# A hybrid decoder block on one core: the first weights' low part in two halves, the fourth early column tile whole

## The chip, the cores and the metric

The kernel runs on one core of a Trainium2 chip. A core has engines that run side by side, each with its own queue of instructions: PE (TensorE) multiplies matrices, DVE (VectorE), ACT (ScalarE) and POOL (GpSimd) work element by element, and SP (SyncE) issues transfers. They wait for each other by semaphores. PE loads 128x128 weights (shown as PEld) and streams the other operand past them; its results go to PSUM, which has banks of 128x512 floats.

The metric is the device time of one execution in microseconds (us); the median of several runs counts.

## The reference

One decoder block with 512 tokens, width 1024, in float32. What is computed, cut to what matters:

```
h = rmsnorm(x, norm1_g)
z = h @ w_in + b_in                                # 1024 x 6656
z_glu, z_rx, z_rg, z_ga, z_gb = split(z)           # 2048, 1280, 1280, 1024, 1024
u = z_glu[:, :1024] * sigmoid(z_glu[:, 1024:])
u = silu(layernorm(causal_depthwise_conv(u, 31 taps)))
y_a = u @ conv_w_out + conv_b_out
xb = causal_depthwise_conv(z_rx, 4 taps)
hb = rg_lru(xb, lru_wa, lru_ba, lru_wx, lru_bx, lru_lambda)   # linear recurrence over the tokens
y_b = (hb * gelu(z_rg)) @ lru_w_out
x = x + (sigmoid(z_ga) * y_a + sigmoid(z_gb) * y_b) @ w_mix_out
h = rmsnorm(x, norm2_g)
x = x + (silu(h @ ffn_w1) * (h @ ffn_w3)) @ ffn_w2             # inner width 2816
out = rmsnorm(x, norm_f_g)
```

The change touches only the first two lines: the normed rows, and the first four column tiles of `z`.

## The kernel before

**Products in three parts.** A float32 operand is split into a high part, rounded to the type that PE multiplies fast (float32r), and a low part, the rest (`split_to`, L131: a copy, then a subtraction at L129). A product is the sum of three matmuls: high weights by high tokens, high weights by low tokens, low weights by high tokens (`mm3`, L530). With `lo_last` all matmuls of the third kind come last.

**Weights.** A column tile of `w_in` is 128 columns wide and 1024 deep, so it has eight pieces of 128x128, numbered c = 0 to 7, side by side in one 128x1024 tile. `wchunk` lists such chunks in the order of use. `load_chunk` issues the transfer into one of four raw buffers (L158); `emit_chunk` (L161) makes the high part and the low part in one of five `hl` buffers, both of them in one tile `hl[P, 2, 1024]`. The high part is made by ACT, for the first chunk by DVE (L172, shown as L133). The low part is made by POOL (L129), for the second chunk by DVE.

**The early stage** (L638 to L669) is under `manual_schedule`: the instructions of PE, ACT, DVE and SP stay in the order in which they are written. POOL's order there, and everything after L669, comes from a planner that goes by its own estimates of when an instruction is ready. The four row tiles of `x` (128 tokens each) are normed (`norm1_rows`, L606), turned by PE (`turn_rows`, L586) and split into high and low parts h1c with norm1_g applied (`turned_parts`, L592: ACT makes the high, DVE the low part of tile c, for 256 tokens at once). While the second half of the tokens is still being prepared, PE already multiplies the first half with four column tiles, those numbered 0, 8, 1 and 9 (`EARLY_IN`; here called in0, in8, in1, in9; they make the first two glu channels). `early_mm(i, hf)` is the product of the i-th of these tiles with half `hf` of the tokens, 24 matmuls of 256 columns, into half of the PSUM bank `z{m}`. The first of them, `early_mm(0, 0)`, has its 24 matmuls in an order written out by hand (L626 and L627, matmuls at L632), because its operands are being made while it runs; the others go through `mm3`. After the four first halves, `rows_turned` (L519) turns the rows of the small parameters, and the four second halves follow.

**After it.** A string of small DVE operations works out the softplus of `lru_lambda` and scaled biases from those parameter rows (L677 to L699, with one Exp on ACT at L680). Then `ORDER` (L226) sets the sequence of the input products, whole column tiles with 24 matmuls of 512 columns, and DVE runs the long convolution beside them (`run_beside`, L789). `glu` takes its early results from `ready`. There are six PSUM banks for products and two for other things.

Of the kernel before, what the change touches and what calls it, by code (L numbers as in the profile page):

```python
# [8 lines left out]
F32 = mybir.dt.float32  # L9
# [17 lines left out]
ND = D // P  # L27
# [69 lines left out]
def tile_block(ctx, tc, a, out):  # L97
# [15 lines left out]
    def pairt(name, dtype=F32R):  # L113

        return longt(f"{name}h", dtype), longt(f"{name}l", dtype)

    def bank(name):
        return psum.tile([P, T], F32, tag="mm", name=name)
# [4 lines left out]
    vec, act, pe, pool_e = nc.vector, nc.scalar, nc.tensor, nc.gpsimd  # L123


    newest = {}

    def sub(eng, o, x, y):
        return eng.tensor_tensor(out=o, in0=x, in1=y, op=ALU.subtract)  # L129

    def split_to(h, l, full, eng, copy=act.copy):  # L131

        copy(h, full)  # L133
        last = sub(eng, l, full, h.bitcast(F32))
        if eng is pool_e:
            newest["sub"] = last.ins
        return h, l
# [8 lines left out]
    emitted = [0]  # L146
# [5 lines left out]
    def load_chunk(i):  # L152
        key, src, kt, cols = chunks[i][:4]
        raw = raws.tile([P, 1024], F32, tag="raw", name=f"raw_{key}")
        if callable(src):
            src(raw)
        else:
            newest["load"] = newest["any"] = nc.sync.dma_start(raw[:, : kt * cols].rearrange("p (k n) -> p k n", k=kt), src).ins  # L158
        loaded_raw[i] = raw

    def emit_chunk():  # L161
        key, src, kt, cols, where, lo, after = chunks[emitted[0]]
        if emitted[0] not in loaded_raw:
            load_chunk(emitted[0])
        raw = loaded_raw.pop(emitted[0])
        emitted[0] += 1
        n = kt * cols
        rv = raw[:, :n]
        if where == "hl":
            hl = hls.tile([P, 2, 1024], F32R, tag="hl", name=f"hl_{key}")  # L170

            h, l = split_to(hl[:, 0, :n], hl[:, 1, :n], rv, lo, act.copy if emitted[0] > 1 else vec.tensor_copy)  # L172
            if after:
                after(rv, h)
            held[key] = (h.rearrange("p (k n) -> p k n", k=kt), l.rearrange("p (k n) -> p k n", k=kt))
        else:
            held[key] = [
                split_to(longt(f"{key}h{i}", F32R), longt(f"{key}l{i}", F32R), rv[:, i * T : (i + 1) * T], lo)
                for i in range(2)
            ]  # L180

    def emit_to(n):
        while emitted[0] < min(len(chunks), n):
            emit_chunk()

    def weights(key, ahead=AHEAD):
        i = next(i for i, c in enumerate(chunks) if c[0] == key)
        emit_to(i + 1 + ahead)
        return held.pop(key)
# [283 lines left out]
    for name, n in ROWS:  # L473
# [4 lines left out]
        while done < n:  # L478
            m = min(n - done, P - row_at(at + done)[1])
# [5 lines left out]
    def load_rows(i):  # L485
        lo, m, src = parts[i]
        b, r = row_at(lo)
        nc.sync.dma_start(rowt[b][r : r + m, :P], src)
# [4 lines left out]
    def load_x(t):  # L493
        for h in range(2):
            nc.sync.dma_start(xt[t][h], x_nat[:, t, h * T : (h + 1) * T])
# [23 lines left out]
    def rows_turned(c0, c1):  # L519
        pt = bank2(f"par_ps{c0}")  # L520
        for c in range(c0, c1, P):
            m = min(P, c1 - c)
            pe.transpose(pt[:, c - c0 : c - c0 + m], rowt[row_at(c)[0]][:m, :P], ident[:m, :m])
        vec.tensor_copy(par[:, c0:c1], pt[:, : c1 - c0])
# [5 lines left out]
    def mm3(ps, ws, xs, lo_last=False):  # L530


        n = 3 * len(ws)
        i = 0
        three = [((wh, xh), (wh, xl), (wl, xh)) for (wh, wl), (xh, xl) in zip(ws, xs)]
        if lo_last:
            three = [q[:2] for q in three] + [q[2:] for q in three]
        for l, r in (q for qs in three for q in qs):
            pe.matmul(ps, l, r, start=i == 0, stop=i == n - 1)  # L539
            i += 1  # L540

    def w_tiles(key, kt, ahead=AHEAD):
        h, l = weights(key, ahead)
        return [(h[:, k, :], l[:, k, :]) for k in range(kt)]
# [41 lines left out]
    def turn_rows(t, ps):  # L586

        for c in range(ND):
            at = 256 * (c // 4) + P * (t % 2)
            pe.transpose(ps[c % 4][:, at : at + P], xt[t][c // 4][:, (c % 4) * P : (c % 4 + 1) * P], ident)  # L590

    def turned_parts(hf, ps):  # L592
        cs = slice(hf * 256, hf * 256 + 256)
        for c in range(ND):
            g, at = pc("norm1_g", c), 256 * (c // 4)
            p_ = ps[c % 4][:, at : at + 256]
            h, l = (v[:, cs] for v in h1p[c])
            act.activation(h, p_, AF.Copy, scale=g)
            vec.scalar_tensor_tensor(out=l, in0=p_, scalar=g, in1=h.bitcast(F32), op0=ALU.mult, op1=ALU.subtract)

    def parts_of(pair_tiles, cs=slice(0, T)):
        return [(h[:, cs], l[:, cs]) for h, l in pair_tiles]

    h1p = [pairt(f"h1{c}") for c in range(ND)]

    def norm1_rows(t, between=lambda: None):  # L606
        junk = [shortt(f"n1j{t}{h}") for h in range(2)]
        r = rstd_of(xt[t], junk)
        for h in range(2):
            vec.tensor_scalar(out=xt[t][h], in0=xt[t][h], scalar1=r, scalar2=None, op0=ALU.mult)  # L610
            if h == 0:
                between()
# [3 lines left out]
    EARLY_IN = [(GLU + j + 8 * o) for j in range(EARLY) for o in range(2)]  # L616
    early = []

    def early_mm(i, hf):
        m = EARLY_IN[i]  # L620
        if hf == 0:
            early.append((m, w_tiles(f"in{m}", ND, 0), bank(f"z{m}")))
        _, ws, ps = early[i]
        if (i, hf) == (0, 0):

            order = [(m, c) for c in range(5) for m in (0, 1)]  # L626
            order += [(2, 0), (2, 1), (0, 5), (1, 5), (2, 2), (2, 3), (0, 6), (1, 6), (2, 4), (2, 5), (0, 7), (2, 6), (2, 7), (1, 7)]  # L627
            xs = parts_of(h1p, HALVES[0])
            for n, (m, c) in enumerate(order):
                (wh, wl), (xh, xl) = ws[c], xs[c]  # L630
                l, r = ((wh, xh), (wh, xl), (wl, xh))[m]
                pe.matmul(ps[:, HALVES[0]], l, r, start=n == 0, stop=n == len(order) - 1)  # L632
            return
        mm3(ps[:, HALVES[hf]], ws, parts_of(h1p, HALVES[hf]), lo_last=hf == 0)


    ET = mybir.EngineType
    with tc.manual_schedule(engines={ET.PE, ET.Activation, ET.DVE, ET.SP}):  # L638

        turned = [bank(f"tx0{q}") for q in range(4)]  # L640
        norm1_rows(0)
        turn_rows(0, turned)
        norm1_rows(1, lambda: rows_turned(0, n_first))
        emit_to(1)
        turn_rows(1, turned)
        turned_parts(0, turned)
        emit_to(2)
        load_x(2)
        load_x(3)
        load_chunk(2)  # L650
        load_chunk(3)
        norm1_rows(2)
        early_mm(0, 0)
        early_mm(1, 0)
        turned = [(bank2, bank)[q // 2](f"tx1{q}") for q in range(4)]
        turn_rows(2, turned)
        norm1_rows(3)
        emit_to(3)
        for i in range(len(parts)):
            if i not in first:  # L660
                load_rows(i)
        turn_rows(3, turned)
        emit_to(4)
        turned_parts(1, turned)
        early_mm(2, 0)
        early_mm(3, 0)
        rows_turned(n_first, n_rows)
        for i in range(4):
            early_mm(i, 1)  # L669
    h1 = parts_of(h1p)  # L670

# [559 lines left out]
    class Seven:  # L1231
# [14 lines left out]
        def copy(self):  # L1246
            self.c11 = shortt(f"c11_{self.k}")
            act.copy(self.c11, self.r1)
# [215 lines left out]
```

## Time and profile before

| | |
|---|---|
| runs | 797.44, 798.24 and 798.44 us; median 798.24 |
| profiled execution | span 797.3 us from its first to its last instruction; the page states no other time of that execution |
| PE busy | 786.5 us (99%) |
| DVE busy | 696.8 us (87%) |
| ACT busy | 473.2 us (59%) |
| POOL busy | 359.9 us (45%) |
| HBM | 231 GB/s over the span |

A row of the timeline has the start, the length, the engine, the source line, the operation and its output and inputs; in brackets stand the idle time before it and what ended that. A row of the chain of waits has the start, the length and what ran. The timeline shows matmuls pipelined, so their lengths overlap; the distance from one start to the next is what a matmul costs. Weight loads (PEld) are shown apart, and their starts show best when PE had to wait. The line of a helper such as `sub` (L129) or the copy in `split_to` (L133) stands for all its callers; tile names tell them apart: `raw_in` and `hl_in` are the chunks of `w_in`.

### The profile page before, as it was taken

Reading aid. Unit: us, or ns where it says so; the run is one execution under the profiler, and the core shown is the slowest. Engines: PE = TensorE matmul, PEld = TensorE weight load, DVE = VectorE, ACT = ScalarE, POOL = GpSimd, SP = SyncE. Lnnn points to the kernel's source line nnn. Section 1 sums busy time; section 2 is a strip of 40 time slices with the busy share of each in tenths; the row PEclk is TensorE's granted clock in tenths of the full one; section 3 lists DMA queues with packets and bytes.
Section 4 is the critical chain, followed back from the end, with each engine's and each line's share of the span. In section 5 each row is a group of like instructions: output and inputs, shape, how many; then the busy total and the mean of one; then the engine's idle time right before and its main releaser. Section 6 shows DMA issues by size and latency. Waiting matters only on the chain.

```text
span 797.3 us, 12582 instructions
## 1 busy us (share of the span) xinstructions
PE 786.5 (99%) x4374; PEld 689.1 (86%) x4374; DVE 696.8 (87%) x1097; ACT 473.2 (59%) x674; POOL 359.9 (45%) x347
## 2 busy tenths in 40 slices
PE   8999999999999999999999999999999999999996
PEld 7988888888888888888887898999999999888885
DVE  5899999999998997985799968898877798999956
ACT  7546688777679654562326467554555555556743
POOL 2576778788779988853360482113312221000000
PEclk9999999999999999999999999999999999999998
DMA  7745566577776786879887887588988898778652
GB/s 216 196 127 175 162 190 195 179 238 229 200 247 202 243 272 212 281 232 296 266 309 238 277 263 230 150 273 264 355 298 289 301 326 294 239 236 258 206 171 105
DMA packets 181074, 188.13 MB, mean 236 GB/s; under 512 B 14119, under 2 KB 142035, under 8 KB 181011
## 3 DMA queue, kind: packets, MB, share of 16 engines
q1 hardware_dynamic: 172195, 156.66, 63.1%
q0 software_dynamic: 8672, 30.41, 11.0%
q8 instruction: 34, 0.56, 0.3%
q10 hardware_dynamic: 144, 0.26, 0.1%
q14 instruction: 29, 0.24, 0.1%
HBM read 145.48 MB, written 38.80 MB: 231 GB/s over the span
## 4 chain that ended last, share of the span: by engine, by line
PE 83%; DVE 9%; DMA 4%; issue 2%; ACT 2%; SPq 0%; DVEq 0%; ACTq 0%
PE z L539 35%; PE fr L1218 24%; PE or L991 13%; PE f L539 3%; PE g L860 3%; PE mxr L991 3%; DMA raw_lo<-in_lru_w_out_dram 1%; DMA raw_co<-in_conv_w_out_dram 1%; DMA mxws<-in_w_mix_out_dram 1%; PE fr L1262 1%; DVE hl_co L129 1%; PE yb L539 1%; DVE hl_mxb L129 1%; DVE mxws L129 1%; DVE sga L1056 1%
## 5 line engine op out<-in xcount | busy, mean ns | idle before, releaser
L733 DVE SCALAR_TENSOR_TENSOR cv<-u,par,cv 128x511 f32<-128x511 f32 (+17 forms) x240 | 162.6, 728 | 1.1 <-ACT cv L730 0.9
L129 POOL TENSOR_TENSOR hl_in<-raw_in,hl_in 128x1024 fp32r<-128x1024 f32 x51 | 123.2, 2422 | 63.6 <-ACT hl_in L133 45.1
L129 POOL TENSOR_TENSOR fws<-fws 128x256 f32<-128x256 f32 x120 | 104.6, 874 | 78.6 <-DMA fws<-in_ffn_w_dram 72.9
L398 POOL DMA_DIRECT2D ot<-fwso x21 | 15.3, 731 | 164.4 <-DVE fwso L129 156.7
L1218 PE MATMUL fr<-hs_0h,hl_ft 128*128 128x256 f32 x320 | 59.2, 283 | 0.0
L133 ACT CAST hl_in<-raw_in 128x1024 fp32r<-128x1024 f32 x51 | 53.2, 1043 | 3.2 <-POOL fws L394 1.3
L129 DVE TENSOR_TENSOR hl_ft<-raw_ft,hl_ft 128x1024 fp32r<-128x1024 f32 x39 | 47.5, 1218 | 5.5 <-ACT hl_ft L133 5.5
L1218 PEld LDWEIGHTS fr<-hs_0h,hl_ft 128*128 128x128 f32 x320 | 50.6, 192 | 0.0
L133 ACT CAST hl_ft<-raw_ft 128x1024 fp32r<-128x1024 f32 x40 | 41.8, 1046 | 13.2 <-PE fr L1218 9.9
L129 DVE TENSOR_TENSOR hl_fb<-raw_fb,hl_fb 128x1024 fp32r<-128x1024 f32 x30 | 36.7, 1222 | 14.6 <-ACT hl_fb L133 13.8
L1218 PE MATMUL fr<-hs_0l,hl_ft 128*128 128x256 f32 x160 | 45.3, 283 | 0.0
L133 ACT CAST hl_fb<-raw_fb 128x1024 fp32r<-128x1024 f32 x30 | 31.5, 1050 | 20.8 <-PE fr L1218 13.3
L539 PE MATMUL z<-h10h,hl_in 128*128 128x512 f32 (+1 forms) x110 | 41.4, 378 | 0.0
L539 PE MATMUL z<-h17h,hl_in 128*128 128x512 f32 (+1 forms) x110 | 41.1, 376 | 0.0
L539 PE MATMUL z<-h11h,hl_in 128*128 128x512 f32 (+1 forms) x110 | 41.1, 376 | 0.0
L539 PE MATMUL z<-h13h,hl_in 128*128 128x512 f32 (+1 forms) x110 | 41.1, 376 | 0.0
L539 PE MATMUL z<-h14h,hl_in 128*128 128x512 f32 (+1 forms) x110 | 41.1, 376 | 0.0
L539 PE MATMUL z<-h15h,hl_in 128*128 128x512 f32 (+1 forms) x110 | 41.1, 376 | 0.0
L539 PE MATMUL z<-h16h,hl_in 128*128 128x512 f32 (+1 forms) x110 | 41.1, 376 | 0.0
L539 PE MATMUL z<-h12h,hl_in 128*128 128x512 f32 (+1 forms) x110 | 41.1, 375 | 0.0
L133 ACT CAST hl_ob<-raw_ob 128x1024 fp32r<-128x1024 f32 (+1 forms) x23 | 23.4, 1016 | 23.4 <-PE or L991 10.5
L394 POOL TENSOR_TENSOR fws<-fws 128x256 f32<-128x256 f32 x40 | 31.6, 792 | 2.8
(962 smaller groups left out, 2640.6 us busy)
## 6 DMA issues: line engine op xcount, KB each, us to landing
raw_in<-in_w_in_dram SPq DMA_DIRECT2D x52, 512.0 KB
fws<-in_ffn_w_dram SPq DMA_DIRECT2D x80, 256.0 KB
raw_ft<-fs SPq DMA_DIRECT2D x34, 512.0 KB
fs<-fws SPq DMA_DIRECT2D x23, 512.0 KB
ot<-fwso POOLq DMA_DIRECT2D x21, 512.0 KB, 6.0
fwso<-in_ffn_w_dram POOLq DMA_DIRECT2D x40, 256.0 KB, 7.1
fs<-fws POOLq DMA_DIRECT2D x17, 512.0 KB, 4.9
raw_ob<-in_ffn_w_dram SPq DMA_DIRECT2D x33, 256.0 KB
```

The source lines that it names most:

```text
L129: return eng.tensor_tensor(out=o, in0=x, in1=y, op=ALU.subtract)
L133: copy(h, full)
L394: eng.tensor_tensor(out=q11, in0=q22, in1=q11, op=ALU.add)
L398: return queue.dma_start(dest, raw.rearrange("p (m n) -> p m n", m=dest.shape[1]))
L539: pe.matmul(ps, l, r, start=i == 0, stop=i == n - 1)
L733: vec.scalar_tensor_tensor(out=acc[c][:, s:], in0=u[c][:, : T - s], scalar=dw(c, s), in1=acc[c][:, s:], op0=ALU.mult, op1=ALU.add)
L860: pe.matmul(ps, l, r, start=k == 0, stop=k == len(mms) - 1)
L991: pe.matmul(banks[i], l_[:, ts], r_, start=start and n == 0, stop=stop and n == 2, skip_group_check=again)
L1056: vec.scalar_tensor_tensor(out=o, in0=ps, scalar=pc("conv_b_out", j), in1=o, op0=ALU.add, op1=ALU.mult)
L1218: pe.matmul(ps[:, HALVES[i]], lw[:, c, :], rx_, start=not (again or i or c or m), stop=bool(i and c == 3 and m == 2), skip_group_check=True,)
L1262: pe.matmul(self.r4[:, HALVES[i]], lw, rx_, start=not (i or c or m), stop=bool(i and c == 3 and m == 2), skip_group_check=True)
```

## The change

The first chunk's high part is still one copy by DVE. Its low part, one subtraction of 128x1024 on POOL, is made by two of 128x512: first the pieces c = 0 to 3, then c = 4 to 7. The hand-written order of the first product is another one: it uses low weights from the seventh matmul on, those of pieces 0 to 3 first. The fourth early column tile (in9) is no longer multiplied in two halves of 24 matmuls with 256 columns each; a new function, `early_whole`, multiplies it with all 512 tokens in 24 matmuls, at the place of its first half. The turning of the parameter rows stands behind it as before, and three second halves follow in place of four.

```diff
--- before.py
+++ after.py
@@ -169,7 +169,13 @@
         if where == "hl":
             hl = hls.tile([P, 2, 1024], F32R, tag="hl", name=f"hl_{key}")
 
-            h, l = split_to(hl[:, 0, :n], hl[:, 1, :n], rv, lo, act.copy if emitted[0] > 1 else vec.tensor_copy)
+            if emitted[0] > 1:
+                h, l = split_to(hl[:, 0, :n], hl[:, 1, :n], rv, lo)
+            else:
+                h, l = hl[:, 0, :n], hl[:, 1, :n]
+                vec.tensor_copy(h, rv)
+                for c in (slice(0, n // 2), slice(n // 2, n)):
+                    newest["sub"] = sub(lo, l[:, c], rv[:, c], h[:, c].bitcast(F32)).ins
             if after:
                 after(rv, h)
             held[key] = (h.rearrange("p (k n) -> p k n", k=kt), l.rearrange("p (k n) -> p k n", k=kt))
@@ -623,8 +629,9 @@
         _, ws, ps = early[i]
         if (i, hf) == (0, 0):
 
-            order = [(m, c) for c in range(5) for m in (0, 1)]
-            order += [(2, 0), (2, 1), (0, 5), (1, 5), (2, 2), (2, 3), (0, 6), (1, 6), (2, 4), (2, 5), (0, 7), (2, 6), (2, 7), (1, 7)]
+            order = [(m, c) for c in range(3) for m in (0, 1)]
+            order += [(2, 0), (2, 1), (0, 3), (1, 3), (2, 2), (2, 3), (0, 4), (1, 4), (0, 5), (1, 5)]
+            order += [(2, 4), (0, 6), (2, 5), (1, 6), (2, 6), (0, 7), (2, 7), (1, 7)]
             xs = parts_of(h1p, HALVES[0])
             for n, (m, c) in enumerate(order):
                 (wh, wl), (xh, xl) = ws[c], xs[c]
@@ -632,6 +639,11 @@
                 pe.matmul(ps[:, HALVES[0]], l, r, start=n == 0, stop=n == len(order) - 1)
             return
         mm3(ps[:, HALVES[hf]], ws, parts_of(h1p, HALVES[hf]), lo_last=hf == 0)
+
+    def early_whole(i):
+        m = EARLY_IN[i]
+        early.append((m, w_tiles(f"in{m}", ND, 0), bank(f"z{m}")))
+        mm3(early[i][2], early[i][1], parts_of(h1p), lo_last=True)
 
 
     ET = mybir.EngineType
@@ -663,9 +675,9 @@
         emit_to(4)
         turned_parts(1, turned)
         early_mm(2, 0)
-        early_mm(3, 0)
+        early_whole(3)
         rows_turned(n_first, n_rows)
-        for i in range(4):
+        for i in range(3):
             early_mm(i, 1)
     h1 = parts_of(h1p)
```

## The prediction

> **What bounds the kernel now.** I read the page first (busy shares and the chain that ended last), then that chain in order of time, then PE's and DVE's waits, then the timelines of the first 38 us.
>
> ```profile
> span 797.3 us, 12582 instructions
> PE 786.5 (99%) x4374; PEld 689.1 (86%) x4374; DVE 696.8 (87%) x1097; ACT 473.2 (59%) x674; POOL 359.9 (45%) x347
> PE 83%; DVE 9%; DMA 4%; issue 2%; ACT 2%; SPq 0%; DVEq 0%; ACTq 0%
> ```
>
> PE is busy for 99% of the span, and 83% of the chain is PE. So a gain has to come from PE's own instructions or from one of PE's few waits. The chain in order of time (start, length, what) shows the early stage:
>
> ```profile
> 10.16 3.89 PE z L632 x23
> 14.05 2.88 PE z L539 x24
> 16.93 1.75 PE tx L590 x16
> 18.68 5.76 PE z L539 x48
> 24.43 0.32 PE par_ps L523 x3
> ...
> 308.78 0.46 PE lnmp L744 x2
> 309.24 10.90 PE z L539 x48
> ```
>
> A product over 256 tokens costs 2.88 us for 24 matmuls, or 0.12 each; over all 512 tokens it is 10.90 / 48 = 0.227 each. The first product (L632) is the slow one: 3.89 for 23. Whatever PE gains here must still be there later, so I looked at who waits (us in total, times, longest):
>
> ```profile
> PE mxr L991 <- DVE x L940: 1.4, 1, 1.4
> DVE z L898 <- ACT z L897: 2.9, 2, 2.2
> DVE u L129 <- ACT lnmp L745: 3.6, 1, 3.6
> ...
> 437.84 0.61 DVE x L940
> 438.50 17.30 PE mxr L991 x75
> ```
>
> The only later stall of PE itself is 1.4 us, at 438.5. The last two lines are the chain there: DVE frees PE. The two DVE waits come from the stretches 200 to 260 and 260 to 330 us: there DVE stands idle until PE's results, passed on by ACT, reach it.
>
> **The change part by part.** I write (0,c), (1,c), (2,c) for high weights x high tokens, high weights x low tokens and low weights x high tokens of input tile c. First the weight loads of the first product, DVE's low parts of the tokens (h1cl), and POOL's subtraction:
>
> ```profile
> 10.94 0.19 PEld L632 LDWEIGHTS z<-h12l,hl_in 128*128 128x128 f32 x1
> 11.05 0.19 PEld L632 LDWEIGHTS z<-h13h,hl_in 128*128 128x128 f32 x1
> 11.73 0.19 PEld L632 LDWEIGHTS z<-h14l,hl_in 128*128 128x128 f32 x1
> 12.11 0.19 PEld L632 LDWEIGHTS z<-h10h,hl_in 128*128 128x128 f32 x1 [0.19 <-POOL hl_in L129]
> 13.65 0.19 PEld L632 LDWEIGHTS z<-h17l,hl_in 128*128 128x128 f32 x1
> 13.77 0.19 PEld L539 LDWEIGHTS z<-h10h,hl_in 128*128 128x128 f32 x1
> ...
> 10.80 0.48 DVE L599 SCALAR_TENSOR_TENSOR h13l<-tx,par,h13h 128x256 fp32r<-128x256 f32 x1
> 11.59 0.48 DVE L599 SCALAR_TENSOR_TENSOR h15l<-tx,par,h15h 128x256 fp32r<-128x256 f32 x1
> 12.37 0.48 DVE L599 SCALAR_TENSOR_TENSOR h17l<-tx,par,h17h 128x256 fp32r<-128x256 f32 x1
> ...
> 9.67 2.38 POOL L129 TENSOR_TENSOR hl_in<-raw_in,hl_in 128x1024 fp32r<-128x1024 f32 x1 [8.36 <-DVE hl_in L133]
> 17.72 4.77 POOL L129 TENSOR_TENSOR hl_in<-raw_in,hl_in 128x1024 fp32r<-128x1024 f32 x2 [5.66 <-ACT hl_in L133]
> ...
> 102.92 1.29 POOL L129 TENSOR_TENSOR hl_gate<-raw_gate,hl_gate 128x512 fp32r<-128x512 f32 x1
> L129 POOL TENSOR_TENSOR hl_gate<-raw_gate,hl_gate 128x512 fp32r<-128x512 f32 x10 | 13.4, 1340 | 5.8 <-DMA raw_gate<-in_lru_wx_dram 4.5 <-ACT hl_gate L133 1.2
> ```
>
> *Low part in halves.* One POOL instruction of 2.38 becomes two of 128x512. The same size elsewhere took 1.29, with a mean of 1.34; an even split, 1.19, is the lower bound. With 1.29 the halves end at 10.96 and 12.25. A wait is seen 0.06 after the end (POOL's 9.67 + 2.38 = 12.05, load at 12.11), so the halves can be used from 11.02 and 12.31. POOL ends 0.20 later, and its next work starts only at 17.72: this costs nothing.
>
> *New order.* Up to (1,2) at 10.94 nothing changes, as DVE paces it. Now (2,0) is the next load, due at 11.05 and ready at 11.02. From there 18 loads follow at 0.12. The tight ones: (1,3) is due at 11.41 and its low part ends at 11.28; (1,5) is due at 12.13 and its low part ends at 12.07; (2,4) is due at 12.25 and ready at 12.31, a stall of 0.06; (1,7) is due at 13.15 and its low part ends at 12.85. So the second product's first load comes at 11.05 + 18 x 0.12 + 0.06 = 13.27 in place of 13.77: 0.50 sooner. With halves of 1.19 to 1.34 it is 0.56 to 0.40. What is late next:
>
> ```profile
> 11.97 1.10 ACT L133 CAST hl_in<-raw_in 128x1024 fp32r<-128x1024 f32 x1
> 16.59 1.05 ACT L133 CAST hl_in<-raw_in 128x1024 fp32r<-128x1024 f32 x1 [0.24 <-DMA raw_in<-in_w_in_dram]
> ...
> 16.58 0.88 DVE L610 TENSOR_SCALAR x<-x,stats 128x512 f32<-128x512 f32 x2
> ...
> 16.66 1.77 PEld L590 LDWEIGHTS tx<-ident,x 128*128 128x128 f32 x16
> 18.41 0.19 PEld L539 LDWEIGHTS z<-h10h,hl_in 128*128 128x128 f32 x1
> 20.31 0.19 PEld L539 LDWEIGHTS z<-h10h,hl_in 128*128 128x128 f32 x1
> ```
>
> The second product's high weights are cast at 13.07, just soon enough. It ends after 2.88, so the 16 transposes begin at 16.15 in place of 16.66. They take 1.75, eight for the third row tile and eight for the fourth. The fourth's rows are scaled by DVE in two halves that end near 17.04 and at 17.46, against a need at 17.03 and 17.47: perhaps 0.1 is lost. The third product (tile in1) then loads at about 18.0, and its first low-weight load, at 20.31 before, falls due at 19.9. But POOL makes that low part from 17.72 to 20.10, after a cast that waited for a DMA and that nothing in this change moves. So the load comes at 20.16, and of the 0.50 only **0.15** is left. This clip makes the size of a POOL half unimportant. Bounds: 0.50 if the clip were not there; 0.03 if all eight transposes waited until 17.5 (17.5 + 0.88 + 1.90 = 20.28).
>
> *Fourth early tile whole.* Two sets of 24 over half the tokens (5.76 for 48) become 24 over all (24 x 0.227 = 5.45): **0.31** saved. Its loads begin at 20.16 + 8 x 0.12 = 21.12. It now needs the second half's low parts while it runs:
>
> ```profile
> 22.42 0.47 DVE L599 SCALAR_TENSOR_TENSOR h17l<-tx,par,h17h 128x256 fp32r<-128x256 f32 x1
> 24.79 0.54 DVE L524 COPY par<-par_ps 128x368 f32<-128x368 f32 x1 [1.89 <-PE par_ps L523]
> 25.99 1.03 ACT L133 CAST hl_in<-raw_in 128x1024 fp32r<-128x1024 f32 x1
> 27.10 4.77 POOL L129 TENSOR_TENSOR hl_in<-raw_in,hl_in 128x1024 fp32r<-128x1024 f32 x2 [4.62 <-ACT hl_in L133]
> 27.18 2.34 DVE L688 TENSOR_TENSOR sm<-sm 128x10 f32<-128x10 f32 x1
> 37.64 0.74 DVE L803 SCALAR_TENSOR_TENSOR u<-z,par,sg 128x512 f32<-128x512 f32 x1
> ```
>
> The last low part is there at 22.89, wanted at 21.12 + 15 x 0.227 = 24.5; the tile's low weights (17.72 + 4.77 = 22.49) are wanted at 24.8. No wait.
>
> By the Trainium skill, page "TensorE: Matmul & The Clock Gate", section "Back-to-back issue gap", one matmul takes N/2.4 + 2.5 ns: 109 ns for 256 columns and 216 for 512. By that the whole tile would save an estimated 24 x (2 x 0.109 - 0.216) = 0.05, and the sum would be 0.2 in place of 0.46. The trace has 0.120 and 0.227, both higher, the narrow one by more, so I keep 0.31.
>
> *Parameter rows moved.* The three transposes at L523 stand behind the whole tile: they load at 21.12 + 5.45 = 26.57, 2.4 after the end of the four half products (18.41 + 48 x 0.12 = 24.17). Behind them move DVE's copy (24.79) and its run of small operations up to L695, ACT's Exp at L680 with the casts queued behind it, and POOL's two subtractions. No DMA is issued by a moved step; SP's loads into the raw buffers that these subtractions free come up to 2.4 later too. Cover: PE goes on with three second halves, 26.57 + 0.33 + 3 x 2.88 = 35.54 (before: four, to 24.17 + 0.33 + 11.52 = 36.02). The next weights' low parts end at 31.87 for two tiles, at most 34.3 then; wanted at 35.54 for the first and 41.0 for the second. DVE's first glu output (37.64) frees its PSUM bank by 40.8; the six banks hold z0, z8, z1, z9, rx0 and rx1, so the next product wants it at 46.4. PE sees nothing. DVE's lag of 2.4 is taken up in its waits for ACT, 2.9 + 3.6.
>
> *Sum.* 0.15 + 0.31 = 0.46 at 36 us. At the 3.6 us wait DVE is released by PE's matmuls at 308.78, so from there its chain, up to the stall at 438.5, moves with PE, and the 0.46 reaches the end. The profiled execution's span 797.3 becomes 796.84. The median of the runs, 798.24, lies 0.94 above that span; 796.84 + 0.94 = **797.8**.
>
> **The rivals.**
> - *DVE's lag stays.* The planner orders DVE after L668 by its own estimate of readiness. If it fills the two waits with other work, the 2.4 us arrive at 437.84. PE is waiting there already, so each us of lag counts in full: 797.3 + 2.4 + 0.94 = 800.6. It beats 0.2% (1.6 us, about what a measurement of this kernel tells from no change) from a lag of 1.6 on. For it: DVE is 87% busy and the small operations are prolonged beside POOL (L688: 2.34 at 27.18). Against it: 6.5 us of waits in between.
> - *The gain ends in the 1.4 us stall.* If the DVE and DMA work before 437.84 keeps its time, PE only waits 1.9 there: 798.2.
> - *The halves are not told apart.* If (2,0) waits for both halves, the load comes at 12.31, and 18 x 0.12 later the second product at 14.47: 0.70 later, less 0.31: 798.6. Against it: high and low part lie in one tile, yet the first product's matmuls start before POOL is done.
> - *The 1.4 us stall goes too,* as the fourth tile's weight buffer and its share of work end 9 us sooner and loads get ahead: 797.8 - 1.4 = 796.4. Nothing in the rows ties these together.
> - *Width is free:* if a wide matmul were paced by its weight load alone, 0.12, the whole tile would save 2.88: 795.2. Against it: 10.90 for 48 at 309.24. The same section of the Trainium skill's page gives 131 ns sustained for 512 columns, which would make it an estimated 3.1 us; the trace's 0.227 contradicts it.
>
> **How the numbers follow.** Forecast 0.42; gain lost in the stall 0.17; halves together 0.05; lag stays 0.22, of which 0.20 beyond 0.2%; stall goes 0.13; width free 0.01. Faster: 0.13 + 0.01 = 0.14. Slower: 0.20. Within 0.2%: the rest, 0.66. The range goes from just under the case with the stall gone, 796.3, up to most of the case with the lag, 800.0; outside lie the top of that case and little below. The forecast's own range is 797.4 (0.50 + 0.31, no clip) to 797.9 (0.03 + 0.31).
>
> **What would show it.** Right: two POOL instructions of about 1.29 from 9.67; the low-weight load at 11.05 without a wait; the second product's first load near 13.3; a new wait of PE's weight load on POOL near 20.1; 24 matmuls of the fourth tile at 0.227; the L523 transposes near 26.6; the first whole-width product after them near 35.5. Wrong: a PE wait between 36 and 437, a wait at L991 longer than about 1.4, or DVE's idle time at 310 gone.

## The result, and the profile after

| | before | after |
|---|---|---|
| median of six runs | 798.34 us (797.44 to 799.42) | 804.98 us (801.51 to 808.46) |
| ratio | 1 | 1.0082, 95% interval 1.006 to 1.0103 |
| profiled execution, span | 797.3 us | 799.7 us |

The change made the kernel 0.8% slower, 6.6 us, where 797.8 was forecast; the range ended at 800.0. A ratio here is worked out from all runs, so it is not quite the quotient of the two medians. The profiled execution of after took 801.51 us, so time less span is 1.8. It was the fastest of its six, and its trace shows only part of the loss of the median.

The page of after, with the answers to the lines shown of before:

```profile
span 799.7 us, 12531 instructions
PE 786.9 (98%) x4350; PEld 687.6 (86%) x4350; DVE 696.0 (87%) x1097; ACT 471.8 (59%) x674; POOL 361.3 (45%) x348
PE 56%; DVE 17%; DMA 8%; POOL 8%; issue 5%; ACT 3%; SPq 2%; POOLq 0%; DVEq 0%; ACTq 0%
```

PE's busy time is as before, within 0.4 us: the loss is idle time of PE. PE's share of the chain that ended last has gone from 83% to 56%; DVE, POOL and DMA have taken the rest.

**The early stage did what was forecast.** The chain of waits of after between 9 and 40 us (start, length, what):

```profile
10.52 3.33 PE z L639 x23
13.85 2.88 PE z L545 x24
16.73 1.85 PE tx L596 x16
18.58 8.34 PE z L545 x48
...
27.24 12.76 PE z L545 x90
```

The tokens landed 0.36 later in this execution, so I measure from the first low-token matmul. The first product takes 3.33, before 3.89. The 48 matmuls at 18.58 are the third tile's first half, 24 at 2.88, and the whole fourth tile in the other 8.34 - 2.88 = 5.46, before 5.76. With three second halves to come the stage ends at 27.24 + 3 x 2.88 = 35.88, 25.36 after its start; before it was 24.75 + 4 x 2.88 - 10.16 = 26.11. So 0.75 was gained against this execution of before.

But that execution was not a typical one. Eight traces of the experiments below have before's first product too. In six of them it took 3.62 or 3.63, not 3.89; in the other two the first weights came late and it took longer. One of the six, before with another sequence up to 97 us (its early stage is before's):

```profile
10.34 3.63 PE z L632 x23
...
24.67 44.19 PE z L539 x240
```

It ends the stage 24.67 + 4 x 2.88 - 10.34 = 25.85 after its start. Against that the change gained 0.49, where 0.46 was forecast.

The timelines of POOL, DVE and PE's weight loads of after in the same stretch:

```profile
9.74 2.53 POOL L129 TENSOR_TENSOR hl_in<-raw_in,hl_in 128x512 fp32r<-128x512 f32 x2 [8.43 <-DVE hl_in L176]
17.73 4.76 POOL L129 TENSOR_TENSOR hl_in<-raw_in,hl_in 128x1024 fp32r<-128x1024 f32 x2 [5.47 <-DMA rows<-in_lru_lambda_dram]
...
11.41 0.19 PEld L639 LDWEIGHTS z<-h10h,hl_in 128*128 128x128 f32 x1
13.57 0.19 PEld L545 LDWEIGHTS z<-h10h,hl_in 128*128 128x128 f32 x1
20.21 0.19 PEld L545 LDWEIGHTS z<-h10h,hl_in 128*128 128x128 f32 x1
...
35.43 2.33 DVE L700 TENSOR_TENSOR sm<-sm 128x10 f32<-128x10 f32 x1
39.93 1.40 DVE L815 SCALAR_TENSOR_TENSOR u<-z,par,sg 128x512 f32<-128x512 f32 x2
41.52 6.04 DVE L745 SCALAR_TENSOR_TENSOR cv<-u,par,cv 128x511 f32<-128x511 f32 x9 [0.19 <-ACT cv L742]
```

The halves are told apart: the first low-weight load comes at 11.41, 0.11 behind that of (1,2), without a wait. The last three rows show DVE. Its first glu output comes 2.3 later (39.93, before 37.64). And the order behind it is another one: both glu outputs run together, then nine operations of the convolution; before, the first glu output was followed by four operations of the convolution, the second glu output and eight more (the first two of these groups are shown):

```profile
39.24 3.12 DVE L733 SCALAR_TENSOR_TENSOR cv<-u,par,cv 128x511 f32<-128x511 f32 x4 [0.85 <-ACT cv L730]
42.26 0.75 DVE L803 SCALAR_TENSOR_TENSOR u<-z,par,sg 128x512 f32<-128x512 f32 x1
```

These two are DVE's timeline of before. The two sequences, listed for the experiments below, say how far this goes. Of DVE's 1,097 instructions 278 stand at another place, of ACT's 603 it is 27, of SP's 569 it is 10; POOL's order differs only by the split subtraction, and PE's not at all behind the early stage. DVE's first difference is the one above, and in the traces its sequences are alike again from about 250 us.

**Where the time is lost.** The weight loads' waits of after, with the total, the number of times and the longest:

```profile
PEld mxr L1003 <- DVE x L952: 2.1, 2, 1.8
PEld mxr L1003 <- ACT mxeb3h L133: 1.5, 1, 1.5
PEld z L545 <- DVE y3l L129: 0.8, 1, 0.8
PEld z L545 <- DVE xb L884: 0.6, 1, 0.6
```

Of before, the same view has after the early stage a single one that counts, at the stall known from the prediction:

```profile
PEld mxr L991 <- DVE x L940: 1.8, 1, 1.8
```

The three new ones come at 198.9, 254.9 and 438.1 us. DVE is late at two of them, and it had been idle before that. The busy time of each engine from 110 to 200 us, first of before, then of after (stretch, its length, then PE, PEld, DVE, ACT, POOL with their instructions, then the granted clock, the share of DMA and GB/s):

```profile
110.00:200.00 90.00, 90.00 (x398) 74.44 (x397) 88.07 (x133) 68.28 (x86) 75.41 (x67) 1.00 0.67 202
```

```profile
110.00:200.00 90.00, 89.62 (x395) 73.77 (x394) 85.65 (x128) 67.68 (x86) 72.23 (x62) 1.00 0.64 195
```

DVE does 2.4 us less work there. Its waits between 100 and 200 us were 1.8 us in all before (first row); after, they are the four that follow:

```profile
DVE hl_gate L218 <- POOL hl_gate L129: 1.8, 2, 1.1
```

```profile
DVE hl_gate L224 <- POOL hl_gate L129: 3.0, 2, 1.9
DVE xb L829 <- ACT xb L827: 1.1, 2, 1.0
DVE cv L745 <- ACT cv L742: 0.8, 1, 0.8
DVE xb L884 <- ACT g L878: 0.5, 1, 0.5
```

That is 5.4 in place of 1.8: in the new order DVE more often comes to an instruction whose input POOL or ACT has not made yet. DVE makes its work up later. From 200 to 320 us, first before, then after:

```profile
200.00:320.00 120.00, 120.00 (x531) 99.27 (x530) 110.64 (x160) 82.13 (x102) 100.35 (x91) 1.00 0.75 231
200.00:320.00 120.00, 119.79 (x528) 98.78 (x527) 114.56 (x167) 81.34 (x101) 99.66 (x89) 1.00 0.73 222
```

At 440 us time is missing again. The chain of before had DVE's x at 437.84 and PE at 438.50. In the chain of after:

```profile
198.93 5.76 PE z L545 x24
...
324.80 5.77 DMA raw_lo<-in_lru_w_out_dram
...
354.18 3.34 DMA raw_lo<-in_lru_w_out_dram
...
439.82 0.61 DVE x L952
...
462.66 10.06 PE fr L1230 x84
```

DVE's x comes 2.0 later. The last row is the first ffn product's; in before it starts at 460.42. That is 2.24 later, and the spans differ by 2.4: nearly all that this execution loses lies ahead of 460 us. Followed back from there, the chain goes through transfers of the output weights (raw_lo is a chunk of `lru_w_out`), through POOL's work and other transfers back to 242.9 us, and through PE back to 198.93, the first of the three new waits. Ahead of that it is DVE in the main, with POOL's hl_gate and a transfer of raw_gate in between. The chain of before is PE alone from 20 us to 326.96. The transfer at 354.18 is on the chain of the kernel with the halves alone as well, which has before's sequence, but there at 349.79:

```profile
349.79 3.46 DMA raw_lo<-in_lru_w_out_dram
```

So by this chain what PE loses at 440 us comes from late weights, and behind them stands the stretch between 110 and 200 us, where POOL too does 3.2 us less work than before. How a wait of PE of 0.8 us at 198.9 becomes 4 us at these transfers is not shown.

The 3.6 us wait at 310, which was to take up DVE's lag, is gone; the other, 2.9 in before, is 4.2. All of DVE's waits of after between 200 and 330 us:

```profile
DVE z L910 <- ACT z L909: 4.2, 2, 3.4
DVE lnmsl L129 <- ACT lnmsh L133: 0.7, 1, 0.7
```

### The profile page after: what moved, and what is told of

Same layout as the page of the kernel before. It is cut to its first block, busy times and chain, and to the rows that moved or that the text cites. A ratio compares the mean times of both kernels' runs of the same rounds, so it can differ in the third digit from the quotient of the medians.

```text
span 799.7 us, 12531 instructions
## 1 busy us (share of the span) xinstructions
PE 786.9 (98%) x4350; PEld 687.6 (86%) x4350; DVE 696.0 (87%) x1097; ACT 471.8 (59%) x674; POOL 361.3 (45%) x348
## 4 chain that ended last, share of the span: by engine, by line
PE 56%; DVE 17%; DMA 8%; POOL 8%; issue 5%; ACT 3%; SPq 2%; POOLq 0%; DVEq 0%; ACTq 0%
PE fr L1230 24%; PE or L1003 13%; PE z L545 11%; DVE cv L745 4%; POOL hl_in L129 4%; POOL fws L129 3%; PE f L545 3%; PE mxr L1003 3%; DMA raw_lo<-in_lru_w_out_dram 2%; DMA fws<-in_ffn_w_dram 2%; DMA fs<-fws 1%; DMA raw_co<-in_conv_w_out_dram 1%; POOL fws L400 1%; PE fr L1274 1%; DVE hl_mxb L129 1%
## 5 line engine op out<-in xcount | busy, mean ns | idle before, releaser
L745 DVE SCALAR_TENSOR_TENSOR cv<-u,par,cv 128x507 f32<-128x507 f32 (+17 forms) x240 | 163.0, 729 | 1.9 <-ACT cv L742 1.7
L129 POOL TENSOR_TENSOR hl_in<-raw_in,hl_in 128x1024 fp32r<-128x1024 f32 (+1 forms) x52 | 123.5, 2382 | 72.4 <-ACT hl_in L133 47.5
```

What stands on the lines that cost most here:

```text
L745: vec.scalar_tensor_tensor(out=acc[c][:, s:], in0=u[c][:, : T - s], scalar=dw(c, s), in1=acc[c][:, s:], op0=ALU.mult, op1=ALU.add)
```

## The experiments

Two theories. *Lag:* the loss comes from DVE being 2.4 us late after the parameter rows. *Order:* it comes from the planner, which sorted the instructions of DVE, ACT and SP after L669 anew because their ready times had moved. To tell them apart I hold a kernel to another one's sequence: ordering edges, which make no engine wait for another, between neighbours in a list of each engine's instructions.

```diff
+    def as_listed(eng, listed):
+        got = [i for i in nc.cur_bb.bb.instructions if i.engine == eng and type(i).__name__ in KINDS]
...
+        info = mybir.DependencyInfo(mybir.DependencyClass.NoSync, mybir.DependencyReason.DATA)
+        for p, q in zip(listed, listed[1:]):
+            tc.add_manual_dep(got[q], got[p].name, info, reason="as_listed")
...
+    as_listed(ET.DVE, LISTED_DVE)
+    as_listed(ET.Activation, LISTED_Activation)
+    as_listed(ET.SP, LISTED_SP)
+    as_listed(ET.Pool, LISTED_Pool)
```

All medians, with the ratio to the runs of before beside which they were made:

| kernel | median us | ratio, 95% interval |
|---|---|---|
| changed, before's sequence | 799.53 | 1.0019, 1.0006 to 1.0031 |
| before, changed sequence | 805.01 | 1.009, 1.0067 to 1.0113 |
| halves alone | 797.60 | 0.9999, 0.9984 to 1.0015 |
| whole tile alone | 805.29 | 1.0086, 1.0054 to 1.0118 |
| changed, rows in mid-tile, before's sequence | 797.92 | 0.9993, 0.9984 to 1.0001 |
| before, rows one product later, before's sequence | 801.10 | 1.0024, 1.0008 to 1.0041 |
| before, second glu output first | 803.19 | 1.0065, 1.0041 to 1.0089 |
| before, changed sequence up to 97 us | 798.55 | 1.0012, 0.9993 to 1.0031 |
| before, changed sequence from 97 us | 805.73 | 1.0083, 1.0059 to 1.0108 |
| before, changed sequence 97 to 168 us | 800.89 | 1.004, 1.002 to 1.0061 |
| before, changed sequence from 168 us | 803.17 | 1.0044, 1.0024 to 1.0064 |

### The changed kernel in before's sequence

The edit is the list above, added to the changed kernel, with before's sequence in it.

> The changed kernel, with the queues of DVE, ACT, SP and POOL behind the early stage held to the sequence that they have in the kernel before (PE keeps the changed kernel's). Theory 'order': the early stage itself gains what was forecast and the loss is the planner's new sequence, so this gives 797.9 (797.4 to 798.4), or a ratio of 0.9990 to 1.0000, and its times scatter by about 2 us as those of before do. Rival 'lag': the parameter rows, turned 2.4 us later, delay DVE whatever the sequence; they are as late here, so this gives 801 to 806 like the changed kernel.

It took 799.53 (798.95 to 802.27), against 798.13 of before. Most of the loss is gone, but 0.19% is left, and its interval leaves out no change: the order is not all of it. All of PE's waits of this kernel between 30 and 450 us, then the matmul in the timeline:

```profile
PE z L545 <- DVE xb L829: 1.9, 1, 1.9
...
109.70 0.47 PE L545 MATMUL z<-h10h,hl_in 128*128 128x512 f32 x1 [1.89 <-DVE xb L829]
```

The chain of waits up to there (95 to 112 us) is DVE alone:

```profile
107.66 0.65 DVE xb L829
...
108.91 0.66 DVE xb L829
...
109.70 2.32 PE z L545 x9
```

And the busy times from 40 to 110 us, DVE's the third:

```profile
40.00:110.00 70.00, 68.11 (x300) 56.03 (x299) 68.24 (x107) 44.10 (x58) 44.69 (x34) 1.00 0.53 153
```

DVE's xb reads an rx product from its PSUM bank, and PE needs that bank for the next product. The wait for this bank comes 69 us behind the first glu output at 40.26, and DVE is busy for 68.24 of the 70 us in between: its idle time there, 1.76 in all, can't take up a lag of 2.5. The last xb starts at 108.82, in before at 106.28, where PE's next product at 107.91 did not have to wait. The stall at 438 us is not there in this execution. An estimate: 1.89 less the 0.49 gained early is 1.4, as far as the two medians lie apart.

### Before in the changed kernel's sequence

The same list with the changed kernel's sequence, added to before; the early stage is before's.

> The kernel before, with the queues of DVE, ACT, SP and POOL held to the sequence of the changed kernel (PE and the early stage as before). 'Order': the loss comes with the sequence alone: 801 to 808, scattered as the changed kernel's times. 'Lag': the parameter rows are as early as in the kernel before, so 798 to 799.

It took 805.01 (803.86 to 808.62): the sequence alone makes the whole loss. The profiled execution, 804.89 us, is close to the median and shows what the fast one of after did not have. Its weight loads' waits:

```profile
PEld mxr L991 <- DVE x L940: 2.2, 2, 1.8
PEld z L539 <- DVE xb L872: 1.4, 1, 1.4
PEld mxr L991 <- ACT mxeb3h L133: 1.2, 1, 1.2
...
PEld ya L539 <- DVE hl_co L129: 1.0, 1, 1.0
```

With three more (1.0 for ACT's hl_co, 0.8 each for DVE's y3l and hl_lo) they sum to 8.4 where before has 1.8 and one of 0.4 charged to issue. PE's own waits, from one matmul to the next, are shorter: 4.9 in all against 1.4. The span is 803.1, 5.8 more than before's, and the first ffn product starts at 466.01, 5.6 later. The three on hl_co and hl_lo are the weights of the branches' output products; they are late here, and PE did not wait for them in the trace of after. The chain of this execution is PE alone from 20 us to 163.9; there it goes over to POOL's hl_gate and hl_in and a transfer of raw_gate. So POOL and the transfers are on the path of the loss, and not DVE alone.

### The halves alone

The changed kernel without the whole tile: the low part in halves and the new order of the first product.

> Only the low part in halves with the first product's new order; the fourth early tile in two halves of tokens as before. The planner gives DVE, ACT and SP the same sequence as in the kernel before. Both theories: the forecast's first term alone, 0.15 us of 798.3 (0 to 0.5), so a ratio of 0.9994 to 1.0000; above 1.002 the halves cost something that neither theory has.

797.60 against 798.13, with an interval that takes in no change (0.9984 to 1.0015). The planner's sequence stays exactly before's. The chain of the early stage:

```profile
9.87 3.32 PE z L639 x23
...
24.00 16.08 PE z L545 x116
```

From 9.87 to 24.00 it is 14.13. Before's profiled execution has 14.59 there, but the typical trace shown above has 24.67 - 10.34 = 14.33: 0.20 gained by 24 us, where the prediction had 0.15. It is too little to be measured in the time.

### The whole tile alone

The kernel before with the fourth early tile whole, and nothing else.

> Only the fourth early tile whole; the low part in one piece and the first product's order as before. The planner gives DVE, ACT, POOL and SP the changed kernel's sequence, and the parameter rows come 2.4 us later. Both theories: 801 to 808, the whole loss of the changed kernel. At 798 the loss would need both parts together.

805.29, ratio 1.0086: the loss belongs to this part. The sequence that the planner makes of it is exactly the changed kernel's. In its chain the third tile's first half and the whole tile take 8.35 together, as in the changed kernel, and the stage ends sooner than before's; the loss comes later.

### The parameter rows one product later, in before's sequence

```diff
         early_mm(3, 0)
+        early_mm(0, 1)
         rows_turned(n_first, n_rows)
-        for i in range(4):
+        for i in range(1, 4):
             early_mm(i, 1)
```

The list with before's sequence is added as well, here and in the next kernel.

> The kernel before with one thing moved: the parameter rows are turned behind the first of the four second halves, 2.9 us later; the queues of DVE, ACT, SP and POOL keep the sequence of the kernel before. 'Lag': DVE runs 2.9 us behind PE, as it does in the changed kernel with the old sequence, so PE waits about 2.3 us near 107 us and the time is 799.3 to 800.5 (1.0015 to 1.003). Rival 'the whole tile itself costs': no whole tile here, so 798.1 and no such wait.

801.10, ratio 1.0024: slower as 'Lag' says, the ratio inside its 1.0015 to 1.003, the median above its 800.5. There is no whole tile and no halved low part in it, and the order is before's; only DVE's run from the parameter rows starts later. Its copy is at 28.60 and its first glu output at 41.44, 3.8 later than before; 0.9 of that is a later start of this execution (its second product is at 14.98, before's at 14.05). The same wait is there, and PE's weight load at 110.86 shows 2.28 of it:

```profile
PE z L539 <- DVE xb L818: 1.9, 1, 1.9
```

So the lag alone costs, and it is the second and smaller cause.

### The parameter rows in the middle of the whole tile, in before's sequence

```diff
-    def mm3(ps, ws, xs, lo_last=False):
+    def mm3(ps, ws, xs, lo_last=False, between=None):
...
+            if between and i == 12:
+                between()
...
-        early_whole(3)
-        rows_turned(n_first, n_rows)
+        early_whole(3, lambda: rows_turned(n_first, n_rows))
```

> The changed kernel with the parameter rows turned in the middle of the whole fourth tile (behind 12 of its 24 matmuls) and the queues of DVE, ACT, SP and POOL held to the sequence of the kernel before. The rows then come 0.3 us sooner than in the kernel before. Theory 'order and lag': with both causes taken away only the forecast's gain is left, 0.46 of 798.1: 797.3 to 798.0, ratio 0.9985 to 1.0000, and PE's wait of 2.3 us near 107 us is gone. Rival 'the whole tile itself costs': 799 to 800, as with the sequence held and the rows late (799.53).

797.92 (796.93 to 798.75), against 798.47: ratio 0.9993, with an interval that just reaches 1.0001. This is the change with both costs removed. Its ratio is the lowest of all, but it is not shown to be faster than before. DVE's copy and first glu output come 0.7 and 0.9 sooner than before's, and the chain keeps the gain. First DVE's timeline, then the chain:

```profile
24.11 0.54 DVE L530 COPY par<-par_ps 128x368 f32<-128x368 f32 x1 [2.33 <-PE par_ps L529]
36.70 0.74 DVE L816 SCALAR_TENSOR_TENSOR u<-z,par,sg 128x512 f32<-128x512 f32 x1
```

```profile
24.08 44.09 PE z L547 x228
```

In this execution (796.93 us, the fastest of its eleven) PE has no wait at all between 30 and 450 us that the view would list.

### One decision of the planner

In before, the first operation of the convolution is put behind the second glu output. That is DVE's first difference between the two sequences.

```diff
+                    with tc.issue_after(u_ins[1]) if (c, s) == (0, 1) else nullcontext():
                         vec.scalar_tensor_tensor(out=acc[c][:, s:], in0=u[c][:, : T - s], scalar=dw(c, s), ...
...
+        u_ins.append(vec.scalar_tensor_tensor(out=uj, in0=pv, scalar=b_in(GLU + j), in1=sg, op0=ALU.add, op1=ALU.mult).ins)
```

> The kernel before with one edge more: the first operation of the long convolution is queued behind the second glu output, as the planner does in the changed kernel by itself; everything after that is the planner's own sequence, which comes out as the changed kernel's but for the place of four convolution operations. Theory 'order': this one decision brings nearly the whole loss, 803 to 806. Rival: the loss needs the early stage's new timing as well: 798 to 800.

803.19, ratio 1.0065. Nothing else was touched; the planner followed with the rest, to a sequence of DVE that in the trace differs from the changed kernel's only in the place of four convolution operations, between 42 and 48 us. One edge at 40 us gives most of the loss. It would cost next to nothing if the rest stayed where it was, as the next run shows.

### Which stretch of the sequence costs

The list again, in before, made of two sequences: the changed one up to or from a point, before's on the other side.

> The early stage of the kernel before; the queues of DVE, ACT, SP and POOL in the changed kernel's sequence up to the end of the first pair of convolution channels (about 97 us), then in that of before. If the close interleaving of the first two channels, and the bank releases that it delays, make the loss: 803 to 806. If the later sequence makes it: 798 to 799.

798.55, ratio 1.0012 (0.9993 to 1.0031): up to 97 us, the first difference included, the new order costs nothing that can be told from no change.

> The reverse: the sequence of before up to the end of the first pair (about 97 us), that of the changed kernel after it, with the early stage of the kernel before. If the later sequence makes the loss (the second pair of convolution channels ended at 174 to 180 us in the changed kernel's trace, against 166 to 168 before): 803 to 806, with PE's waits near 199, 255 and 440 us. If the first 97 us make it: 798 to 799.

805.73, ratio 1.0083: all of it lies after 97 us. I divided that part once more, at 168 us, where before's second pair of convolution channels ends.

> The early stage of the kernel before; the changed kernel's sequence only for what the kernel before queues between the ends of the first and the second pair of convolution channels (about 97 to 168 us); ACT's sequence comes out as before there, so this is in the main DVE's. If the loss comes from the second pair's operations queued later on DVE: 803 to 806, with the second pair ending near 175 to 180 us. If it comes after that: 798 to 799.

> As before up to the end of the second pair (about 168 us), the changed kernel's sequence of DVE, ACT and SP after it. If the loss comes from there: 803 to 806, with the second pair ending near 168 us as before. If from the stretch before it: 798 to 799.

800.89 and 803.17, ratios 1.004 and 1.0044. The loss is in neither stretch alone: the two add up to 0.84%, the 0.83% of the whole, each with an interval of 0.2% to either side. I had expected all of it from one of the two. The first run fits neither case; the median of the second is just inside 803 to 806, but its ratio is half the loss. ACT's copy at the end of the second pair's last channel shows the first half of it, for before:

```profile
168.37 0.59 ACT L736 COPY u<-cv 128x512 f32<-128x512 f32 x1 [0.48 <-DVE cv L733]
```

and for after, where it comes 11 us later:

```profile
179.68 0.59 ACT L748 COPY u<-cv 128x512 f32<-128x512 f32 x1
```

With the new order from 97 to 168 alone it comes at 173.29, with the new order from 168 on at 170.05. So a late pair goes with the loss of the first stretch and can't be the loss of the second. DVE's stretch from 110 to 200 us has 87.17 us of work in the first and 84.97 in the second of these kernels, against 88.07 in before: each has gaps of its own. Which instruction of each stretch makes them is open; one engine's new order with the other engines' old was not tried.

## Why the prediction was wrong

- *Low part in halves, new order:* close in size, **0.20** measured for **0.15**, but by another account, so this is luck. The second product's first load comes 13.57 - 10.52 = 3.05 behind the first low-token load. In before's profiled execution it was 13.77 - 10.15 = 3.62, but in the six typical traces it is 3.33 to 3.35: the new order saves 0.30, not 0.50. The transposes lose 0.11 of it (their loads take 1.88 for 1.77; the forecast had "perhaps 0.1"). The clip to 0.15 at the third tile's low part takes nothing: the load at 20.21 comes without a wait, 0.04 after it can. POOL starts on that low part 7.21 after the first low-token load, and so it does, to 0.01, in ten of the twelve traces other than before's, of both kinds of early stage. In before's it was 7.57, and only there did the cast ahead of it wait for its transfer. The forecast took both from that one execution.
- *Fourth tile whole:* right. 5.46 measured for 5.45, 0.30 gained for **0.31**. The rule of the Trainium skill's page "TensorE: Matmul & The Clock Gate", section "Back-to-back issue gap", 216 ns for 512 columns, would make it an estimated 5.18; the trace has 0.227 each and does not agree. Both widths lie above that rule by the same 0.011, the narrow one not by more, and two narrow matmuls pay it twice.
- *Parameter rows moved:* **this step failed**, twice. "PE sees nothing" went by the first reuse of a bank, at 46.4, which is indeed not late. But it took DVE's lag to be harmless until DVE's waits behind 200 us take it up. With before's sequence the lag reaches PE at 109.7, through a later bank, since DVE is busy for 68.2 of the 70 us from 40 to 110. Alone this costs 0.2%.
- The larger miss is in the same step. It followed each moved instruction in before's sequence, though everything after L669 is sorted by ready times, and the step moves these by 2.4 us. It put no price on another sequence. The runs show that this is the loss: 0.9% with the sequence and no other change, 0.19% with the change and the old sequence.
- *The rival "DVE's lag stays"* named the planner, with a chance of 0.22 and a time of 800.6. Its condition came true: the wait at 310 was filled, and the stall at 438 grew. Its price did not: it counted the lag alone. The new order has waits of its own: DVE's between 110 and 200 us, and those for late weights behind 320 us.
- *The rival "the 1.4 us stall goes too"* is not shown. In the mid-tile kernel no wait of PE at L1004 is listed. But with the halves alone, where no tile is whole, PE's wait there is 0.4 as well, and before with the changed sequence up to 97 us has the same 0.4. So the 1.4 of before's profiled execution is nothing that before's sequence always has. *"Halves not told apart"* and *"width is free"* are refuted by the rows above.
- *The base:* 0.94 was added to the span. In every other profiled execution here, time less span is 1.7 to 1.9, so before's, span 797.3, took an estimated 799.1 and was one of its slower ones; its early stage and its stall at 438 show why. That puts the forecast 0.9 too low against its own execution, and explains nothing of the 6.6.

## What to carry to other kernels

A change that moves when a planner's instructions become ready also moves their order, far behind the place of the edit: compare the instruction sequences of the two kernels first, and if they differ, hold the new kernel to the old sequence to see what the edit itself is worth. An engine that has no gap ahead of it hands a lag on: look for the first stretch in which it is full and for what it frees there, a PSUM bank here, and not for the first place where it waits. Small early gains (0.5 us of 798) are worth less than the order of what follows (0.8%): here they show in the trace with the order and the start of DVE's run both as before, and even then not for certain in the time. And one profiled execution is one sample: a wait of a few tenths in it (0.24 for a transfer, 1.4 at 438 us) can be its own, so look for it in a second trace before a forecast rests on it.

## What was not expected of the hardware

Short DVE operations of 128x10 take 0.17 us, but 2.33 beside POOL's subtraction (at 35.43 in the trace of after, with a subtraction from 35.34 for 2.39), as in before: one such operation is as long as the whole lag. POOL's two halves took 2.53 for what took 2.38 in one, 0.15 for the second instruction. And the changed kernel scatters more: its six runs span 7.0 us, the 23 of before beside the first experiments 4.5 (797.37 to 801.83), though the 20 beside later ones span 6.7. What sets this is open; that PE waited for hl_co and hl_lo in one execution and not in another suggests transfers, but no run tests it.
